# Weight halves read twice from DRAM by GpSimd's DMAs, and the residual put into PSUM ahead of the down products

## The chip, the cores and the metric

The kernel runs on one core of a Trainium2 chip. The metric is device time in microseconds (us) of one execution, lower is better. The core's engines run side by side, each through a queue of its own in a fixed order: TensorE (PE, matmuls and transposes), ScalarE (ACT), VectorE (DVE), GpSimd (POOL) and SyncE (SP), which here only issues DMAs. An instruction waits at the head of its engine's queue for what it reads or overwrites, and everything behind it on that engine waits with it. DMAs are moved by 16 DMA engines that all queues share.

## The reference

The reference is a decoder of two layers on 256 tokens of width 2048, in float32. Each layer projects the normalised x once, runs two groups of attention heads side by side (gated linear attention and stick-breaking attention), adds the output projection to x, and then adds an MLP of width 8192 with a squared ReLU:

```python
h = rms_norm(x, attn_norm)
proj = jnp.einsum('bsd,de->bse', h, w_in)
g_q, g_k, g_v, g_gate, g_lr, s_q, s_k, s_v = jnp.split(proj, COL_SPLITS, axis=-1)
...
mixed = jnp.concatenate([o_gla, o_sb], axis=-1)
x = x + jnp.einsum('bse,ed->bsd', mixed, w_o)
hm = rms_norm(x, mlp_norm)
up = jnp.square(jax.nn.relu(jnp.einsum('bsd,df->bsf', hm, w_up)))
return x + jnp.einsum('bsf,fd->bsd', up, w_down)
```

The weights `w_in`, `w_o`, `w_up` and `w_down` of both layers, some 400 MB, are read from DRAM in float32, and nearly all of the time goes into their products with 256 tokens.

## The kernel before

**Products.** A float32 product is made of three faster ones. An operand `w` is split into a high part, `w` rounded to the type fp32r, and a low part, `w` less the high part; the product is high by high, high by low and low by high (lines L1121, L1122 and L1123 in `product`, L594 to L596 in `unit`). So each matmul has three rows in the profile, on tiles `whi`, `wlo` or `dlo` (weights, high and low) and `act` (activations).

**Units and pairs.** Away from the attention the work is cut into units of 256 tokens by 1024 output columns. In a layer they are g (the gate), o twice (output projection), then four times up, up, down, down, and, ahead of each layer's attention, `iv`, `ik` and `iq`, three parts of that layer's input projection (`layer_units`). A unit runs over eight pairs; a pair is 256 rows by 1024 columns of weights, 1 MB, which SP loads into a tile `raw` in DRAM's layout (L981). ScalarE makes the high parts (L1008, `high`), VectorE the low parts (L1012, `low`), in halves of 128x1024 each.

**Fast and added pairs.** Pairs 1, 3, 5 and 6 (`FAST`) take seven products in place of eight, by Strassen and Winograd; their sums of weights are VectorE's (L840, tiles `ts`). Pairs 2 and 7 (`ADDED`) spare VectorE the low part: ScalarE writes the negated high part into a tile `dlo` (L1018, a copy with scale −1 that rounds), and a DMA of GpSimd adds `raw` onto it, from SBUF to SBUF (L1021). ScalarE makes their high part as well, so an added half costs it two instructions. There are 38 units with added pairs, 152 halves.

**PSUM and tails.** Products are summed in eight banks, called m1 to m8 by number. When a unit ends, `down_tail` or `up_tail` empties the banks. A down unit or an o unit adds its sums to the residual x, which stays in SBUF as `xb`: twelve VectorE additions on 128x512 (L840), among them those that read `xb` and write it. An up unit's tail applies the squared ReLU and turns the result for the next products (ScalarE L1185 and L1213 among others).

**What sets the order.** Inside `ordered` (called before layer 0 and once a layer), ScalarE's and VectorE's instructions are put in order by `Plan`, a list scheduler with a length for each piece of work and due times counted from TensorE's order. TensorE, SP and GpSimd keep the order in which the program adds their work. Outside it (the opening product of GV, `unit` with operands from `operand_parts`, L471 to L494; and the attention) the order is the program's. Tiles come in rings: 5 of `whi`, 4 of `wlo`, 2 of `dlo`, 5 of `raw`.

**Two places.** At the start SP loads x in four pieces between weights (L356, L309 gains, L564 weights), TensorE transposes x (L471) with idle transposes of `ident` ahead of it (L544), and ScalarE scales the result to the first operand (L481). At the end of each layer's attention ScalarE and VectorE finish a head norm (squares L662, VectorE's sum L663, statistics L386 and L387), while unit g's first weights come in.

Of the kernel before, what the change touches and what calls it, by code (L numbers as in the profile page):

```python
# [14 lines left out]
ALU = mybir.AluOpType  # L15
# [6 lines left out]
STEPS = [0, 0, 1, 1, 1, 2, 3, 1, 3, 2, 3, 3, 4, 4, 5, 5, 6, 5, 5, 6, 6, 6, 7, 7]  # L22
LOADS = [0, 1, 2, 3, 4, 5, 6, 7]
FAST = (1, 3, 5, 6)
FEWER = [0, 0, 1, 1, 1, 2, 3, 1, 3, 2, 3, 3, 4, 4, 5, 5, 6, 6, 6, 6, 7, 7], (1, 3, 6)
ADDED = (2, 7)
# [21 lines left out]
class Plan:  # L48
# [10 lines left out]
    class Piece:  # L59
        def __init__(self, engine, length, fn, deps, lag):  # L60
            self.engine, self.length, self.fn, self.lag = engine, length, fn, lag
            self.deps = deps
            self.users = []
            self.after = []
# [4 lines left out]
    def add(self, engine, length, fn, *deps, lag=0.0):  # L69
        flat = []  # L70
        for d in deps:
            flat.extend(d if isinstance(d, (list, tuple)) else [d])
        self.pieces.append(Plan.Piece(engine, length, fn, [d for d in flat if d], lag))
        return self.pieces[-1]

    def run(self):
# [25 lines left out]
        order, events, count = [], [], 0  # L102
        for p in self.pieces:
            if not p.deps:
                events.append((0.0, count, p))
                count += 1
        came = set()
        while events:
            now, _, p = heapq.heappop(events)
# [6 lines left out]
            for e in free:  # L116
                if free[e] > now + 1e-9:
                    continue
                if e in ready:
                    if not ready[e]:  # L120
                        continue
                    p = heapq.heappop(ready[e])[2]
# [6 lines left out]
                heapq.heappush(events, (free[e], count, None))  # L129
                count += 1  # L130
                for u in p.users:
# [4 lines left out]
                    if not left[u]:  # L136
                        heapq.heappush(events, (at[u], count, u))
                        count += 1
# [8 lines left out]
def trunk_kernel(  # L147
# [59 lines left out]

    ATT = ("wg", "ident16", "mask16", "tri", "nones", "gmask", "reset", "v4", "lr", "lrT", "ha", "hh", "hl", "hA", "on", "dec", "S", "kdz", "row", "bc", "eg")
    MLP = ("whi5", "dlo", "sxh", "sx", "ts", "raw2")
# [213 lines left out]
    def forms(op, i, t, tag):  # L423

        keep = tag is None
# [16 lines left out]
        def high():  # L442
            if e:
                if keep:
# [378 lines left out]
    def ordered(l, units, hT, rst, ug, gates_t, mixed=None, ons=None):  # L823
# [11 lines left out]
        RING, LOWS, ADDS, RAWS = 5, 4, 2, 5  # L835
# [11 lines left out]
        def unit_order(u):  # L847

            kind, _, n2 = units[u]
            if kind == "g":  # L850
                return [i // 2 for i in range(8)], ()
            if kind == "o":
                pairs = ((4, 5, 6, 7, 0, 1, 2, 3), (4, 5, 6, 0, 7, 1, 2, 3))[n2]
                return [j for j in pairs for _ in range(4 if j < 2 else 2)], (0, 1)
            return FEWER if u and units[u - 1][0] == "down" and kind == "iv" else (STEPS, FAST)

        def step_banks(u, j, is_fast):
# [4 lines left out]
            if kind in BIG and j in ADDED and not by_columns(u, j):  # L862
# [24 lines left out]
        def squares(n, ss):  # L887
            return add("ACT", 2 * A1, lambda: norm_squares(n, ss), x_done[n])
# [23 lines left out]
        def made(f, got, tag_fast, first):  # L912
# [9 lines left out]
            if tag_fast:  # L922
                e = add("DVE", 1.25, lambda: part(0), first)
            b = add("ACT", A1 * (2 if tag_fast else 1), lambda: part(1), e)
            return add("DVE", 1.1 if tag_fast else V1, lambda: part(2), b)

        def turned(n, h2, m, op, key, ll, sums=False):
# [4 lines left out]
            if sums and fast(i):  # L932
                box = []
                b = add("ACT", A1, lambda: box.append(scaled()), a)
                free[m] = [b]
                return made(
                    lambda: forms(op, i, box[0], None if op is hT else "sxh"), None, True, b
# [23 lines left out]
        def load(u, i):  # L961
# [4 lines left out]
            def fn():  # L966
                if x % RAWS >= RAWS - 2:
                    box.append(tmp("raw2", [P, 2, 1024], bufs=2))
# [21 lines left out]
        def by_columns(u, i):  # L990

            return units[u][0] in BIG and i in ADDED and i == unit_order(u)[0][-1]

        def high_tile():
            if len(whi) % RING == 0:
                return lambda: tmp("whi5", [P, 2, 512], F32R, bufs=1)
            return lambda: ppool.tile([P, 2, 512], F32R, tag="whi", name=nm("whi"), bufs=RING - 1)

        def parts(src, readers, deps, n=2, by_dma=False):
# [16 lines left out]
            def negated():  # L1016
                box["l"] = tmp("dlo", [P, 2, 512], F32R, bufs=ADDS)
                nc.scalar.activation(box["l"], src(), AF.Copy, scale=-1.0)  # L1018

            def add_weights():  # L1020
                nc.gpsimd.dma_start(f32(box["l"]), src(), accum_op=ALU.add)  # L1021

            if by_dma:
                m = add("ACT", A2, negated, deps, dlo[-ADDS] if len(dlo) >= ADDS else [])
                lo = add("POOL", 2.7, add_weights, m, lag=ADD)
                dlo.append([])
                readers.extend((m, lo))
            h = add("ACT", A2 if n == 2 else A1, high, deps, whi[-RING], last.get("h"))
            whi.append([])
            if not by_dma:  # L1030
                lo = add("DVE", V2 if n == 2 else V1, low, h, wlo[-LOWS], last.get("l"))
                last["l"] = lo
                wlo.append([])
                whi[-1].append(lo)
                readers.append(lo)
            last["h"] = h
            readers.append(h)
            return box, h, lo, [whi[-1], (dlo if by_dma else wlo)[-1]]

        last = {}  # L1040
        sums13 = []


        def steps(u, j, is_fast, r, ld, readers):
# [16 lines left out]

            def ext(i):
# [693 lines left out]
```

## Time and profile before

| what | before |
|---|---|
| median of 3 runs | 2133.17 us (2133.06 to 2133.46) |
| profiled execution, its own span | 2131.6 us |
| TensorE busy | 2123.5 us |
| VectorE busy | 1929.5 us |
| ScalarE busy | 1535.1 us |
| GpSimd busy | 152.1 us |
| read from DRAM | 405.12 MB |

The profile is that of one execution. A row of its groups names the line, the engine, the operation, the tiles (output from input, numbers left out), their shapes and the count; then the busy time, the mean of one in ns, and the idle time just before them with what ended most of it. A row of the timeline gives the start in us, the busy time, engine, line and tiles, and in brackets the idle time ahead of it with its releaser. A row of the waits gives engine and tile, the releaser, the sum, the count and the longest. PEld is the loading of weights into TensorE beside its matmuls. "SPq" and "POOLq" mark DMAs that these engines issue.

### The profile page before, as it was taken

The numbers are of one execution on the slowest core, as the hardware profiler recorded it, in microseconds if no ns is written. First come the engines' busy times: TensorE is split into PE (matmuls) and PEld (weight loads), VectorE is DVE, ScalarE is ACT, GpSimd is POOL, SyncE is SP. The second block draws the span as 40 slices with busy tenths as digits, with TensorE's granted clock in tenths as the row PEclk, the third lists the DMA queues.
The fourth block names the chain that finished last, engine by engine and source line by source line (L and its number), as shares of the span: only waits on it lengthen the run. The fifth ranks groups of instructions, "written<-read, shape, count | busy, mean of one in ns | idle before, by whom it ended". The sixth has DMA issues, their size and how long they took to land.

```text
span 2131.6 us, 28370 instructions
## 1 busy us (share of the span) xinstructions
PE 2123.5 (100%) x10094; PEld 1768.9 (83%) x10094; DVE 1929.5 (91%) x2598; ACT 1535.1 (72%) x1989; POOL 152.1 (7%) x210
## 2 busy tenths in 40 slices
PE   9999999999999999999999999999999999999999
PEld 7888888888888888888888888888888888888887
DVE  6988779999999999999998886799999999999998
ACT  7777666777677677677777665667876776776775
POOL 0010000000000000000000100000000000000000
PEclk9999999999999999999999999999999999999999
DMA  8975355688888888878888644657888888888886
GB/s 287 265 203 182 115 198 178 217 242 264 249 247 252 249 256 249 269 237 254 238 260 252 178 138 136 201 186 219 262 234 267 245 261 250 246 254 248 254 252 178
DMA packets 156114, 488.76 MB, mean 229 GB/s; under 512 B 9690, under 2 KB 18466, under 8 KB 155972
## 3 DMA queue, kind: packets, MB, share of 16 engines
q1 hardware_dynamic: 134084, 407.25, 55.9%
q0 software_dynamic: 21888, 79.70, 19.7%
q8 instruction: 79, 1.29, 0.2%
q14 instruction: 63, 0.52, 0.1%
HBM read 405.12 MB, written 2.10 MB: 191 GB/s over the span
## 4 chain that ended last, share of the span: by engine, by line
PE 96%; DVE 2%; ACT 1%; issue 0%; DMA 0%; DVEq 0%; ACTq 0%
PE acc L594 3%; PE acc L596 3%; PE acc L595 3%; DVE wlo L1012 0%; PE ps L1693 0%; PE ps L1686 0%; DVE wlo L577 0%; PE ps L705 0%; PE ps L1643 0%; PE ps L759 0%; PE ps L723 0%; DMA dlo<-raw 0%; DVE t L1548 0%; PE ps L471 0%; PE ps L771 0%
## 5 line engine op out<-in xcount | busy, mean ns | idle before, releaser
L1008 ACT ACTIVATE whi<-raw 128x1024 fp32r<-128x1024 f32 (+1 forms) x847 | 814.9, 976 | 344.5 <-issue 48.2
L1012 DVE TENSOR_TENSOR wlo<-raw,whi 128x1024 fp32r<-128x1024 f32 (+1 forms) x695 | 757.6, 1097 | 88.3 <-ACT whi L1008 76.0
L1021 POOL DMA_DIRECT2D dlo<-raw x152 | 129.4, 852 | 1733.7 <-ACT dlo L1018 921.1
L1008 ACT ACTIVATE whi<-ts 128x1024 fp32r<-128x1024 f32 x159 | 168.6, 1060 | 80.0 <-DVE ts L840 5.8
L1012 DVE TENSOR_TENSOR wlo<-ts,whi 128x1024 fp32r<-128x1024 f32 x159 | 193.9, 1219 | 11.1 <-ACT whi L1008 8.4
L840 DVE TENSOR_TENSOR ts<-raw 128x1024 f32<-128x1024 f32 x159 | 194.0, 1220 | 2.7 <-DMA raw<-in_w_in_dram 0.9
L1018 ACT ACTIVATE dlo<-raw 128x1024 fp32r<-128x1024 f32 x152 | 155.3, 1044 | 3.6 <-PE m__2021_9487 L1122 1.7
L594 PE MATMUL acc<-whi,act 128*128 128x512 f32 (+2 forms) x384 | 141.3, 368 | 0.0
L596 PE MATMUL acc<-whi,act 128*128 128x512 f32 (+2 forms) x384 | 136.9, 356 | 0.0
L595 PE MATMUL acc<-wlo,act 128*128 128x512 f32 (+2 forms) x384 | 136.7, 356 | 0.0
L575 ACT ACTIVATE whi<-raw 128x1024 fp32r<-128x1024 f32 (+2 forms) x98 | 88.5, 908 | 63.7 <-PE acc L596 63.0
L577 DVE TENSOR_TENSOR wlo<-raw,whi 128x1024 fp32r<-128x1024 f32 (+2 forms) x98 | 100.4, 1031 | 33.2 <-ACT whi L575 33.1
L840 DVE TENSOR_TENSOR raw<-raw 128x512 f32<-128x512 f32 x159 | 109.4, 688 | 2.7
L840 DVE TENSOR_TENSOR raw<-ts,raw 128x512 f32<-128x512 f32 x159 | 108.9, 685 | 0.7
L594 PEld LDWEIGHTS acc<-whi,act 128*128 128x128 f32 x384 | 72.6, 189 | 12.3 <-issue 3.4
L596 PEld LDWEIGHTS acc<-whi,act 128*128 128x128 f32 x384 | 72.4, 189 | 10.5
L595 PEld LDWEIGHTS acc<-wlo,act 128*128 128x128 f32 x384 | 72.6, 189 | 8.9 <-DVE wlo L577 0.2
L1213 ACT ACTIVATE act<-act,st 128x512 f32<-128x512 f32 x88 | 60.3, 712 | 25.9 <-DVE act L840 25.9
L456 DVE TENSOR_TENSOR act<-t,act 128x512 fp32r<-128x512 f32 x88 | 59.8, 683 | 0.0
L452 ACT ACTIVATE act<-t 128x512 fp32r<-128x512 f32 x88 | 54.3, 621 | 0.4 <-DVE t L440 0.3
L840 DVE TENSOR_TENSOR xb<-t,xb 128x512 f32<-128x512 f32 x40 | 27.3, 682 | 0.1
L663 DVE TENSOR_REDUCE st<-t 128x4 f32<-128x512 f32 (+1 forms) x36 | 21.8, 619 | 5.7 <-ACT t L662 5.5
(3399 smaller groups left out, 5605.6 us busy)
## 6 DMA issues: line engine op xcount, KB each, us to landing
raw<-in_w_up_dram SPq DMA_DIRECT2D x112, 1024.0 KB, 6.3
raw<-in_w_down_dram SPq DMA_DIRECT2D x112, 1024.0 KB, 6.3
raw<-in_w_in_dram SPq DMA_DIRECT2D x78, 1024.0 KB, 5.5
dlo<-raw POOLq DMA_DIRECT2D x152, 512.0 KB, 6.5
raw<-in_w_o_dram SPq DMA_DIRECT2D x32, 1024.0 KB, 5.1
raw<-in_w_up_dram SPq DMA_DIRECT2D x32, 512.0 KB, 6.7
raw<-in_w_down_dram SPq DMA_DIRECT2D x32, 512.0 KB, 6.5
raw<-in_w_in_dram SPq DMA_DIRECT2D x26, 512.0 KB, 6.4
```

The costliest lines, as they stand in the source:

```text
L456: nc.vector.tensor_tensor(d[:, :, 1, :], src, f32(d[:, :, 0, :]), ALU.subtract)
L575: newest["hi"] = nc.scalar.activation(h, r, AF.Copy).ins
L577: newest["lo"] = nc.vector.tensor_tensor(lo[:, q : q + step, :width], r, f32(h), ALU.subtract).ins
L594: nc.tensor.matmul(o, xh[:, sl], whi[:, j, :width], start=first, stop=False)
L595: nc.tensor.matmul(o, xh[:, sl], wlo[:, j, :width], start=False, stop=False)
L596: st["mm"] = nc.tensor.matmul(o, xl[:, sl], whi[:, j, :width], start=False, stop=last).ins
L840: nc.vector.tensor_tensor(dst, a, b, op)
L1008: nc.scalar.activation(box["h"][:, :n], src(), AF.Copy)
L1012: nc.vector.tensor_tensor(box["l"][:, :n], src(), f32(box["h"][:, :n]), ALU.subtract)
L1018: nc.scalar.activation(box["l"], src(), AF.Copy, scale=-1.0)
L1021: nc.gpsimd.dma_start(f32(box["l"]), src(), accum_op=ALU.add)
L1213: nc.scalar.activation(box[h][:, tt, :], box[h][:, tt, :], AF.Relu if into else AF.Copy, scale=(rr if into else st["rst"])[:, tt : tt + 1],)
```

## The change

**Added pairs.** A half of an added pair is no longer loaded by SP. GpSimd's DMAs read it from DRAM twice: once with a cast to fp32r into a tile `chi`, which is the high part, and once, after ScalarE has written the negated `chi` into `dlo`, adding the weights from DRAM onto it. So ScalarE's high instruction is gone for the 152 halves, SP issues fewer loads (by the order, 96 of 1 MB for up and for down in place of 112), GpSimd's DMAs go from 152 to 304, and the DRAM read grows by the second reading to some 485 MB. `chi` has a ring of 3, `raw` one of 3 in place of 5; GpSimd queues the next half's `chi` ahead of a half's addition (`AHEAD_BY`). The added pairs are now 2 and 4, and their two halves are no longer neighbours in the order of steps (`EACH`).

**Seeds.** In the eight down units of a layer and the second o unit (`SEEDED`), 18 in all, ScalarE copies the four residual tiles of `xb` into banks 2, 4, 3 and 8 before the unit's first products there, which then add onto them. The tail is eight VectorE instructions in place of twelve.

**The scheduler** also counts the temporary tiles `t2` now: a piece that takes one is held until one is left (`take`, `sure`, `give`).

```diff
-STEPS = [0, 0, 1, 1, 1, 2, 3, 1, 3, 2, 3, 3, 4, 4, 5, 5, 6, 5, 5, 6, 6, 6, 7, 7]
-ADDED = (2, 7)
+EACH = [0, 0, 1, 1, 1, 1, 2, 3, 3, 3, 3, 2, 5, 5, 5, 5, 4, 6, 6, 6, 6, 4, 7, 7], FAST, (2, 4)
+SEEDED = (("down", 0), ("down", 1), ("o", 1))
+CAST, AHEAD_BY = 3, 1
+RING, LOWS, ADDS, RAWS = 5, 4, 2, 3
...
-                if by_columns(u, i):
-                    for c in range(2):
-                        nc.sync.dma_start(
-                            dst[:, c, :].rearrange("p (k n) -> p k n", k=2),
-                            src[:, :, c * 512 : (c + 1) * 512],
-                        )
-                else:
-                    nc.sync.dma_start(dst, src)
+                nc.sync.dma_start(dst, src)
...
+        def rounded(u, j, s):
+            box = {}
+            sl = slice(s * 512, (s + 1) * 512)
+            src = weights(u, j)[:, :, sl] if by_columns(u, j) else weights(u, j)[:, s : s + 1, :]
...
+            def high():
+                box["h"] = tmp("chi", [P, 2, 512], F32R, bufs=CAST)
+                nc.gpsimd.dma_start(flat("h"), src)
+            def negated():
+                box["l"] = tmp("dlo", [P, 2, 512], F32R, bufs=ADDS)
+                nc.scalar.activation(box["l"], f32(box["h"]), AF.Copy, scale=-1.0)
+            def add_weights():
+                nc.gpsimd.dma_start(flat("l"), src, accum_op=ALU.add)
+            users = [[], []]
+            h = add("POOL", 1.0, high, chi[-CAST] if len(chi) >= CAST else [], lag=LAND)
+            chi.append(users[0])
+            if len(late) >= AHEAD_BY:
+                late.pop(0)()
...
+            def rest():
+                m = add("ACT", A2, negated, h, dlo[-ADDS] if len(dlo) >= ADDS else [])
+                dlo.append(users[1])
+                got[2] = add("POOL", 1.0, add_weights, m, lag=ADD)
+            late.append(rest)
...
+        def seed(m, x):
+            banks[m] = bank(m)
+            nc.scalar.activation(banks[m], x(), AF.Copy)
+        def seeded_tail(u):
...
+            seeds = {
+                m: add("ACT", A1, lambda m=m, x=x: seed(m, x), free[m], x_done.get(2 * n2 + c))
+                for m, x, c in ((2, x11, 0), (4, x21, 0), (3, x12, 1), (8, x22, 1))
+            }
```

Three places of the order of instructions, each before and after. Lines have moved: L481 is now L500, L494 is L513, L575 is L594, L1008 is L1066, L662 is L681, L386 and L387 are L402 and L403, L880 is L903. New are L1033 (the load `chi`), L1037 (the negation) and L1040 (the addition).

GpSimd's queue at the start of the program, before; `dlo` are the low parts of added halves:

```order
masks.py:197 MEMSET ident 128x128
masks.py:199 ISA
masks.py:199 AFFINE_SELECT ident<-ident 128x128
L1021 DMA dlo_457<-raw_400 128x1024
L1021 DMA dlo_467<-raw_400 128x1024
L1021 DMA dlo_648<-raw_558 128x1024
```

and after:

```order
masks.py:197 MEMSET ident 128x128
L1033 DMA chi_398<-in_w_in_dram 128x1024
masks.py:199 ISA
masks.py:199 AFFINE_SELECT ident<-ident 128x128
L1033 DMA chi_400<-in_w_in_dram 128x1024
L1040 DMA dlo_406<-in_w_in_dram 128x1024
L1033 DMA chi_413<-in_w_in_dram 128x1024
L1040 DMA dlo_408<-in_w_in_dram 128x1024
```

The first load of `chi` now stands between the two instructions that make `ident`, and two loads and the first addition come right behind.

ScalarE at the start, before; `act` is the operand of the opening product, `whi` its weights' high parts:

```order
L241 ACT_TABLE_LOAD
L481 ACTIVATE act_122<-ps_109,gcol_a 128x256 x2
L481 ACTIVATE act_127<-ps_114,gcol_a 128x256 x2
L575 ACTIVATE whi_151<-raw_146 128x512 x2
L575 ACTIVATE whi_159<-raw_146 128x512 x2
```

and after:

```order
L257 ACT_TABLE_LOAD
L1037 ACTIVATE dlo_406<-chi_398 128x1024
L1037 ACTIVATE dlo_408<-chi_400 128x1024
L500 ACTIVATE act_122<-ps_109,gcol_a 128x256 x2
L500 ACTIVATE act_127<-ps_114,gcol_a 128x256 x2
L594 ACTIVATE whi_151<-raw_146 128x512 x2
L594 ACTIVATE whi_159<-raw_146 128x512 x2
```

Two negations, which wait for the first two loads of `chi`, moved to the head of the queue, ahead of the first operand.

ScalarE at the end of layer 0's attention, before; `raw_2917` holds unit g's first weights:

```order
L784 ACTIVATE act_2712<-ps_2834 128x512
L1008 ACTIVATE whi_622_2925<-raw_2917 128x1024
L662 ACTIVATE t_591_2847<-act_2712 128x512
L386 ACTIVATE st_2851<-st_2850 128x4
L387 ACTIVATE st_2851<-st_2851 128x4
L880 ACTIVATE act_2896<-acc_2610,st_393 128x512
L1008 ACTIVATE whi_2930<-raw_2917 128x1024
```

and after:

```order
L803 ACTIVATE act_2697<-ps_2819 128x512
L681 ACTIVATE t_585_2832<-act_2697 128x512
L402 ACTIVATE st_2836<-st_2835 128x4
L403 ACTIVATE st_2836<-st_2836 128x4
L1037 ACTIVATE dlo_2912<-chi_2904 128x1024
L1037 ACTIVATE dlo_2914<-chi_2906 128x1024
L1066 ACTIVATE whi_619_2917<-raw_2902 128x1024
L903 ACTIVATE act_2881<-acc_2595,st_393 128x512
```

The first high of unit g moved from ahead of the squares to behind the statistics and two negations. Layer 1 has the same rows at its place.

More of the change, by code (lines that the diff above doesn't have):

```diff
@@ L1028, in parts @@
             h = add("ACT", A2 if n == 2 else A1, high, deps, whi[-RING], last.get("h"))
             whi.append([])
[L1030 to L1035, printed above, removed]
+            lo = add("DVE", V2 if n == 2 else V1, low, h, wlo[-LOWS], last.get("l"))
+            last["l"] = lo
+            wlo.append([])
@@ L1036, in parts @@
+            whi[-1].append(lo)
+            readers.append(lo)
             last["h"] = h
             readers.append(h)
-            return box, h, lo, [whi[-1], (dlo if by_dma else wlo)[-1]]
+            return box, h, lo, [whi[-1], wlo[-1]]
         last = {}
         sums13 = []
+        chi, late, made_halves = [], [], {}
+        every = [
+            (u, k, j, order[:k].count(j))
+            for u in range(len(units))
+            for order, _, by_dma in [unit_order(u)]
+            for k, j in enumerate(order) if j in by_dma
+        ]
@@ L1129, in down_tail @@
         def down_tail(u):
[L1130 to L1131 removed]
+            n2 = units[u][2]
             x11, x21, x12, x22 = (
```

270 lines of the change are left out of this document (179 added, 91 removed).

## The prediction

> **What bounds the kernel now.** I read first the page's head and busy times, then the windows over single stretches, then the waits of TensorE, and last the timeline where the windows or waits leave a gap.
>
> ```profile
> span 2131.6 us, 28370 instructions
> PE 2123.5 (100%) x10094; PEld 1768.9 (83%) x10094; DVE 1929.5 (91%) x2598; ACT 1535.1 (72%) x1989; POOL 152.1 (7%) x210
> ```
>
> Windows of the start, the first unit of the list scheduler and a long stretch of the MLP (columns: window, its length, busy us and instructions of PE, PEld, DVE, ACT, POOL, granted clock, DMA share, GB/s):
>
> ```profile
> 0.00:10.00 10.00, 7.90 (x32) 6.77 (x33) 2.41 (x6) 4.69 (x9) 0.70 (x6) 1.00 0.74 223
> 10.00:20.00 10.00, 10.00 (x53) 8.46 (x52) 7.63 (x14) 8.04 (x20) 0.00 (x0) 1.00 1.04 394
> 34.00:75.00 41.00, 40.49 (x174) 31.81 (x173) 39.28 (x57) 32.38 (x40) 3.64 (x4) 1.00 0.84 239
> 700.00:1100.00 400.00, 400.00 (x1814) 332.18 (x1813) 380.28 (x487) 302.01 (x372) 31.92 (x38) 1.00 0.83 248
> ```
>
> All the waits of TensorE that the profile counts:
>
> ```profile
> PE ps L544 <- POOL ident masks.py:199: 1.4, 1, 1.4
> PE ps L705 <- DVE act L668: 1.1, 2, 0.5
> PE ps L471 <- DMA xb<-in_x_dram: 0.7, 1, 0.7
> PE m__79_428 L1122 <- DMA dlo<-raw: 0.3, 1, 0.3
> PE m__4043_18997 L1121 <- DVE xb L840: 0.2, 1, 0.2
> ```
>
> TensorE is the bound: from 700 to 1100 us it is busy 400.00 of 400.00 us, at the full granted clock, and outside that it waits 3.7 us in all. The matmuls are the same in number and shape before and after. So no saving on ScalarE, VectorE or SP can shorten the time by more than TensorE's idle, 2131.6 − 2123.5 = 8.1 us, most of which lies at the very start. What can happen is that something arrives late. I therefore price the work saved at nothing and look for what becomes late.
>
> **The work taken away.** Rows of the page's groups for the instructions that change in number (the DMA's row is its issue on GpSimd):
>
> ```profile
> L1008 ACT ACTIVATE whi<-raw 128x1024 fp32r<-128x1024 f32 (+1 forms) x847 | 814.9, 976 | 344.5 <-issue 48.2
> L1021 POOL DMA_DIRECT2D dlo<-raw x152 | 129.4, 852 | 1733.7 <-ACT dlo L1018 921.1
> L1018 ACT ACTIVATE dlo<-raw 128x1024 fp32r<-128x1024 f32 x152 | 155.3, 1044 | 3.6 <-PE m__2021_9487 L1122 1.7
> L840 DVE TENSOR_TENSOR xb<-t,xb 128x512 f32<-128x512 f32 x40 | 27.3, 682 | 0.1
> ```
>
> ScalarE loses the 152 highs of the added halves (152 × 0.976 = 148 us); it gains 72 copies of the residual into PSUM, at about 0.58 us (the PSUM copy of L1185 below) 42 us. VectorE loses 72 × 0.682 = 49 us from the tails of 18 units. GpSimd issues 304 DMAs in place of 152, 0.85 us each, on an engine that is busy 7% of the time. Both lie beside a full TensorE: worth 0. The few early waits that more room on these engines may remove are 0.5 us (40.49 of 41.00 busy in 34:75) and the 0.2 us at the last unit: −0.7 us.
>
> **The transfers.** The queues' rows (packets, MB, share of 16 engines) and the landing times of two kinds of DMA (KB, us from issue to landing):
>
> ```profile
> q1 hardware_dynamic: 134084, 407.25, 55.9%
> q0 software_dynamic: 21888, 79.70, 19.7%
> raw<-in_w_up_dram SPq DMA_DIRECT2D x112, 1024.0 KB, 6.3
> dlo<-raw POOLq DMA_DIRECT2D x152, 512.0 KB, 6.5
> ```
>
> A half is 0.524 MB. As an SP load it takes all 16 engines 0.559 × 2131.6 / 407.25 × 0.524 = 1.53 us; as an accumulate 0.197 × 2131.6 / 79.70 × 0.524 = 2.76 us. The trace has no casting load from DRAM (`chi`); I bound it by these two, 1.53 and 2.76 us, and take the lower, since it reads DRAM and writes SBUF as the SP load does and reads no destination. The accumulate now reads DRAM in place of SBUF; I leave it at 2.76. A half then costs 4.29 us as before, at most 5.52; at four halves in a unit of some 41 us the DMA share goes from 0.83 to between 0.83 and 0.95. Under 1: worth 0 in the steady part, if each half is asked for early enough. GpSimd queues one half ahead, so within a 41 us unit halves are wanted every 7 us or so; reckoning the chain (`chi` landing, negation 1.04 us, accumulate landing) at 6.5 us a landing, the last accumulate is there about 3.6 us before its product. I take 0. Upper end: with a cast as dear as an accumulate, a wait of some 0.5 us in each of the 38 units that have added pairs, 19 us.
>
> Three raw buffers in place of five: an SP load now waits for the last reader three loads back. In the order of a unit pair 5's load waits for pair 0's last read, some 2.7 us into the unit; with 6.3 us to land it is there at 9 us, and wanted at 12 to 14 us: 0.
>
> **The seeds.** A seeded unit may not start a bank before ScalarE has copied the residual into it. At the end of a down unit's predecessor, near 2000 us:
>
> ```profile
> 1994.56 0.58 ACT L1185 ACTIVATE act<-m__3813_17928 128x512 f32<-128x512 f32 x1
> 1997.56 0.68 DVE L840 TENSOR_TENSOR act<-m__3799_17862,act 128x512 f32<-128x512 f32 x1
> 2000.55 0.68 DVE L840 TENSOR_TENSOR act<-m__3802_17875,act 128x512 f32<-128x512 f32 x1
> 2000.87 0.39 PE L1121 MATMUL m__3868_18198<-whi,act 128*128 128x512 f32 x1
> 2002.23 0.39 PE L1121 MATMUL m__3871_18211<-whi,act 128*128 128x512 f32 x1
> ```
>
> Bank 2 is read out at 1998.24 and written again at 2000.87, a slack of 2.6 us; bank 4 at 2001.23 and 2002.23, 1.0 us. A copy of 0.58 us fits both, so 0. If ScalarE is in another instruction of 1 us, bank 4 is late by half a microsecond: at most 18 × 0.5 = 9 us, the upper end.
>
> **The start.** The first rows of GpSimd's queue now are `chi` loads, and ScalarE's first two instructions are the negations of two of them, ahead of the operand that opens the first product. Rows of SP's queue, ScalarE and TensorE at the start of before:
>
> ```profile
> 0.82 0.95 SPq L356 DMA_DIRECT2D xb<-in_x_dram  x2
> 1.82 0.46 SPq L309 DMA_DIRECT2D t<-in_attn_norm_dram  x1
> 2.32 1.85 SPq L564 DMA_DIRECT2D raw<-in_w_in_dram  x4
> 4.21 0.43 SPq L356 DMA_DIRECT2D xb<-in_x_dram  x1
> ...
> 6.54 1.57 ACT L481 ACTIVATE act<-ps,gcol_a 128x256 fp32r<-128x256 f32 x4 [4.44 <-DVE gcol_a L319]
> ...
> 1.44 1.97 PE L544 MATMUL ps<-ident 128*128 128x128 f32 x8 [1.44 <-POOL ident masks.py:199]
> ...
> 6.21 3.04 PE L544 MATMUL ps<-ident 128*128 128x128 f32 x13
> 8.90 0.78 PE L594 MATMUL acc<-whi,act 128*128 128x512 f32 x1
> ...
> 12.40 1.03 PE L471 MATMUL ps<-ident,xb 128*128 128x128 f32 x8
> ```
>
> Two things can hold it up. First GpSimd and ScalarE: `chi` issues of 0.85 us stand before and behind the two instructions that make `ident`, which comes 0.85 later; the 8 warm transposes then end at 4.26, and x's transposes, at 4.07 before, lose 0.2, which lies inside what follows. The second `chi` is issued at about 2.2 us; if it lands as GpSimd's DMAs do in the middle of the kernel, 6.5 us less the 1.4 by which a load takes the engines shorter than an accumulate (2.76 − 1.33, below), at 7.3, its negation ends at 8.4, where the operand began at 6.54: +1.8. (Had it landed by 4.4 us, nothing would be lost.) Second the shared engines: the windows show 2.23 MB moved by 10 us at 223 GB/s, and the second piece of x, with 2.1 MB ahead of it or in it, comes just then; TensorE transposes it at 12.40, a slack of 2.4 us. Now three `chi` (3 × 1.33 us, 0.524 MB at the 394 GB/s of 10:20) and two accumulates (2 × 2.76) can share the engines with it: 9.5 us. If they take turns, x comes at 19.5 and TensorE is held by 19.5 − 12.4 = +7.1 us. If SP's stream goes first, 2.1 MB of x and gains and 3.15 MB of weights, 17.6 us by the same rates with the 0:10 window's, the two `chi` and the negation end at 17.6 + 2 × 1.33 + 1.04 = 21.3, and ScalarE's operand is late by +14.8. Between 0 and +14.8 I take +7.1, as both queues have work from 2 us on and nothing in the trace shows one of them held back.
>
> The Trainium skill, "DMA: Bandwidth & Descriptors", section "Queues, rings and completion order", says that each DMA engine goes round its queues packet by packet; by that rule the two streams take turns and the term is 7.1, not 14.8. No run here shows it yet. The Trainium skill, "TensorE: Matmul & The Clock Gate", "Part 1: The HAM clock gate", has the array fall to half rate after about 3.4 us of idleness; the trace agrees in the start, where 13 transposes took 3.04 us and 8 later ones 1.03. By that page, as an estimate, a hold of 7 us would cost half of 3.4, some 1.7 us, more, and the sum would read 2143.5.
>
> **The two ends of attention.** `chi` shares memory with the attention's tiles, so each `ordered` begins with fresh halves. In both layers two negations stand ahead of the first high of unit g (the order above). The timeline of before there:
>
> ```profile
> 284.64 1.05 ACT L1008 ACTIVATE whi<-raw 128x1024 fp32r<-128x1024 f32 x1
> 285.59 0.62 ACT L662 ACTIVATE t<-act 128x512 f32<-128x512 f32 x1
> ...
> 288.03 0.21 ACT L387 ACTIVATE st<-st 128x4 f32<-128x4 f32 x1
> ...
> 285.73 1.23 DVE L1012 TENSOR_TENSOR wlo<-raw,whi 128x1024 fp32r<-128x1024 f32 x1 [2.02 <-ACT whi L1008]
> ...
> 289.63 0.39 PE L1121 MATMUL m__629_2942<-whi,act 128*128 128x512 f32 x1
> 289.86 0.39 PE L1122 MATMUL m__629_2942<-wlo,act 128*128 128x512 f32 x1
> ...
> 1347.71 0.39 PE L1121 MATMUL m__2660_12490<-whi,act 128*128 128x512 f32 x1
> ```
>
> The high at 284.64 was 5 us ahead of TensorE. Now it follows L387's counterpart. Without high and low ahead of them, the squares of L662 and VectorE's sum come about 1.5 us earlier, so the statistics end at 288.24 − 1.5 = 286.7; two negations (2.09) end at 288.8, the high at 289.85, the low 1.23 later at 291.1, where the product read it at 289.86: +1.25, less what the matmul before it covers, +1.1. Were the statistics not earlier, +2.6. Twice: +2.2 (2 to 5). The negations themselves wait for `chi` loads that are issued when the attention's last tiles are free, some 280 us, landing at about 286.7: just in time.
>
> **The sum.** 2131.6 + 7.1 + 2.2 − 0.7 = 2140.2. This execution's span stands 1.6 us below the median of 2133.17 (2133.06 to 2133.46), so 2141.8 us, 0.4% slower. What a measurement can tell here is about 0.2%, 4.3 us: 2128.9 to 2137.4 is no change.
>
> **The rivals.** B, SP's stream goes first at the start: 2131.6 + 14.8 + 2.2 − 0.7 + 1.6 = 2149.5. For it: SP issues half a dozen loads before GpSimd's first; against it: loads and accumulates ran beside each other all through the MLP. C, not slower: the first two `chi` land by 4 to 5 us and x is not pushed past its slack, so the start costs nothing: 2131.6 + 2.2 − 0.7 + 1.6 = 2134.7. For it: in 0:10 the DMA share was only 0.74 and the accumulates come late, after a landing and a negation; it decides when the start costs under 2.8 us. D, the cast is as dear as the accumulate or the chain of three steps too slow: the start costs 5 × 2.76 − 2.4 = 11.4, that is 2146, and with up to 0.5 us in 38 units 2165, its middle about 2152. For it: the 6.5 us to landing is a median with little behind it (slack 3.6 us); against it: a share of at most 0.95.
>
> **The chances.** The likeliest case, the turns at the start, 0.45 (its own range 2138 to 2147); C 0.22; D 0.20; B 0.13. Faster by over 0.2% would need 4.3 us of TensorE's 8.1 us idle, of which 0.7 is within reach: 0.03. Same takes most of C: 0.20. Slower 0.77. The range leaves out the lowest part of C and the upper half of D: 2134 to 2156.
>
> **What would show it.** ScalarE's first instructions after would be two `dlo<-chi` that wait for DMAs, and the first `act<-ps` after 6.54 us; TensorE's wait on `ps<-xb` would be about 7 us. In unit g of both layers the first product with `wlo` would come 1 to 2 us after the statistics' old place, with a wait on VectorE's low. In 700:1100 TensorE would still be at 400 of 400 with a DMA share of 0.83 to 0.95. If it shows waits on `dlo` or on `xb` copies into the banks instead, D or the seeds' upper end is right. A `chi` load that lands in 3 us at the start would make the forecast too high; a share at 1.0 too low.

## The result and the profile after

The changed kernel takes 2150.07 us (median of four runs, 2148.3 to 2156.37) against 2133.28 us before: the ratio is 1.0085, with an interval of 1.0070 to 1.0099. That is slower by 0.85%, inside the forecast's range and twice as far from the kernel before as its 2141.8 us. The runs before lie within 0.4 us of each other, those after within 8 us. The profiled execution after has a span of 2146.6 us.

The head of the page, the two queues and the landing times of the changed kernel:

```profile
span 2146.6 us, 28212 instructions
PE 2127.6 (99%) x10094; PEld 1768.6 (82%) x10094; DVE 1886.1 (88%) x2526; ACT 1436.8 (67%) x1909; POOL 234.6 (11%) x362
...
q1 hardware_dynamic: 103076, 327.55, 44.3%
q0 software_dynamic: 43776, 159.40, 31.2%
...
raw<-in_w_up_dram SPq DMA_DIRECT2D x96, 1024.0 KB, 10.2
chi<-in_w_up_dram POOLq DMA_DIRECT2D x64, 512.0 KB, 6.8
dlo<-in_w_up_dram POOLq DMA_DIRECT2D x64, 512.0 KB, 9.4
```

VectorE lost 43 us of work and ScalarE 98 us, and neither moved the end. TensorE has the same 10094 rows and 4 us more of busy time (products right after a wait take longer); its idle time grew from 8.1 to 19.0 us. The additions land 9.4 us after their issue where they took 6.5, and SP's loads of 1 MB 10.2 where they took 6.3.

TensorE's waits after:

```profile
PE acc L613 <- ACT whi L594: 3.7, 1, 3.7
PE ps L563 <- POOL ident masks.py:199: 2.5, 1, 2.5
PE ps L490 <- DMA xb<-in_x_dram: 1.4, 1, 1.4
PE m__3274_15522 L1202 <- DMA dlo<-in_w_down_dram: 1.1, 1, 1.1
PE m__3882_18394 L1202 <- DMA dlo<-in_w_down_dram: 1.1, 1, 1.1
...
PE m__626_2935 L1202 <- DVE wlo L1070: 0.8, 1, 0.8
PE m__2619_12388 L1202 <- DVE wlo L1070: 0.8, 1, 0.8
...
PE m__1279_6067 L1202 <- DMA dlo<-in_w_down_dram: 0.6, 1, 0.6
```

Three groups are new or longer: the start (the first three rows), the first low of unit g in each layer (0.8 us twice), and additions that come late (`dlo`). How much each costs is read at marks that both programs have. TensorE's order between them holds the same work, so the difference of two times is the delay collected so far. The marks are the end of the opening product on ScalarE, the first gate product of each layer's attention on TensorE, and the last matmul. Before:

```profile
34.36 0.60 ACT L880 ACTIVATE act<-acc 128x512 f32<-128x512 f32 x1 [3.13 <-PE acc L596]
...
186.84 1.13 PE L1536 MATMUL ps<-lrT,wg 17*128 17x256 f32 x4
1223.36 1.13 PE L1536 MATMUL ps<-lrT,wg 17*128 17x256 f32 x4
2127.19 0.39 PE L1123 MATMUL m__4048_19021<-whi,act 128*128 128x512 f32 x1
```

and after:

```profile
42.20 0.60 ACT L903 ACTIVATE act<-acc 128x512 f32<-128x512 f32 x1 [3.63 <-PE acc L615]
...
195.28 1.13 PE L1676 MATMUL ps<-lrT,wg 17*128 17x256 f32 x4
1235.12 1.13 PE L1676 MATMUL ps<-lrT,wg 17*128 17x256 f32 x4
2142.10 0.39 PE L1203 MATMUL m__3972_18829<-whi,act 128*128 128x512 f32 x1
```

The delay is 42.20 − 34.36 = 7.8 us at the end of the opening, 8.4 at the first gate product, 11.8 at the second and 14.9 at the end. So half of it is collected in the first 42 us and the rest in small pieces.

**The start.** ScalarE, TensorE and the queues of the changed kernel (the last three rows are the window from 13.80 to 17.30 us, in the columns of the prediction's windows, and the queues' shares in the first 24 us):

```profile
8.32 1.06 ACT L1037 ACTIVATE dlo<-chi 128x1024 fp32r<-128x1024 f32 x1 [6.22 <-DMA chi<-in_w_in_dram]
10.73 1.06 ACT L1037 ACTIVATE dlo<-chi 128x1024 fp32r<-128x1024 f32 x1 [1.35 <-DMA chi<-in_w_in_dram]
11.69 1.55 ACT L500 ACTIVATE act<-ps,gcol_a 128x256 fp32r<-128x256 f32 x4
...
13.81 0.51 PE L613 MATMUL acc<-whi,act 128*128 128x512 f32 x1 [3.70 <-ACT whi L594]
15.56 0.63 PE L613 MATMUL acc<-whi,act 128*128 128x512 f32 x1
15.99 0.63 PE L614 MATMUL acc<-wlo,act 128*128 128x512 f32 x1
18.59 1.04 PE L490 MATMUL ps<-ident,xb 128*128 128x128 f32 x8
23.77 1.09 PE L490 MATMUL ps<-ident,xb 128*128 128x128 f32 x8 [1.40 <-DMA xb<-in_x_dram]
...
13.80:17.30 3.50, 3.27 (x8) 2.39 (x9) 3.28 (x6) 2.35 (x5) 0.00 (x0) 0.55 1.07 262
...
q1 hardware_dynamic: 2543, 4.25, 53.3%
q0 software_dynamic: 720, 2.62, 42.0%
```

The two negations at the head of ScalarE's queue wait for `chi` until 8.3 and 10.7 us, and the first operand is made at 11.69 in place of 6.54. The first matmul comes at 13.81 in place of 8.90, 4.9 us late. TensorE has then waited 3.7 us and runs its next products 0.43 us apart (15.56 to 15.99) where 0.23 is its pace, at a granted clock of 0.55: 13.81 to 18.59 takes 4.8 us where 8.90 to 12.40 took 3.5, another 1.3 us, of which 0.2 is a wait for a low part. The third piece of x adds 1.4. The two queues share the engines, 53% and 42%, and landings stretch: SP's first weights (256 KB) take 8.1 us where they took 5.2 (and 5.4 in e2 below, which holds the `chi` loads back).

**The first low of unit g.** At the end of layer 0's attention:

```profile
295.15 1.99 ACT L1037 ACTIVATE dlo<-chi 128x1024 fp32r<-128x1024 f32 x2
297.04 1.04 ACT L1066 ACTIVATE whi<-raw 128x1024 fp32r<-128x1024 f32 x1
...
298.12 1.23 DVE L1070 TENSOR_TENSOR wlo<-raw,whi 128x1024 fp32r<-128x1024 f32 x1 [1.57 <-ACT whi L1066]
...
299.40 0.50 PE L1202 MATMUL m__626_2935<-wlo,act 128*128 128x512 f32 x1 [0.76 <-DVE wlo L1070]
```

The two negations run on ScalarE from 295.15, the high follows at 297.04 and the low at 298.12, and TensorE waits for it. From 8.51 (298.14 against 289.63, the product ahead) the delay goes to 9.54 (299.40 against 289.86).

**A late addition.** GpSimd's queue and TensorE near 690 us:

```profile
684.76 0.55 POOL L1033 DMA_DIRECT2D chi<-in_w_down_dram  x1 [5.69 <-PE m__1284_6092 L1202]
686.84 0.85 POOL L1040 DMA_DIRECT2D dlo<-in_w_down_dram  x1 [1.53 <-ACT dlo L1037]
...
696.67 0.50 PE L1202 MATMUL m__1279_6067<-dlo,act 128*128 128x512 f32 x1 [0.65 <-DMA dlo<-in_w_down_dram]
```

The `chi` load of the next half and the negation of this half wait for products of the same finished half, since `chi` has three buffers and `dlo` two. So the load is issued 2 us ahead of the addition, in the same queue, and the addition lands 9.8 us after its issue (696.67 − 686.84), later than TensorE wants it.

### The profile page after: what moved, and what is told of

It is laid out like the page before. It is cut to its first block, busy times and chain, and to the rows that moved or that the text cites. A ratio compares the mean times of both kernels' runs of the same rounds, so it can differ in the third digit from the quotient of the medians.

```text
span 2146.6 us, 28212 instructions
## 1 busy us (share of the span) xinstructions
PE 2127.6 (99%) x10094; PEld 1768.6 (82%) x10094; DVE 1886.1 (88%) x2526; ACT 1436.8 (67%) x1909; POOL 234.6 (11%) x362
## 3 DMA queue, kind: packets, MB, share of 16 engines
q0 software_dynamic: 43776, 159.40, 31.2%
## 4 chain that ended last, share of the span: by engine, by line
issue 47%; PE 42%; POOL 6%; DMA 2%; DVE 1%; ACT 1%; SPq 0%; POOLq 0%
POOL dlo L1040 3%; PE acc L613 3%; PE acc L615 3%; PE acc L614 3%; POOL chi L1033 2%; DMA dlo<-in_w_down_dram 1%; DMA xb<-in_x_dram 1%; DMA raw<-in_w_up_dram 1%; DVE wlo L596 0%; PE ps L724 0%; PE ps L1833 0%; PE ps L778 0%; PE ps L1783 0%; PE ps L1826 0%; PE ps L742 0%
## 5 line engine op out<-in xcount | busy, mean ns | idle before, releaser
L1066 ACT ACTIVATE whi<-raw 128x1024 fp32r<-128x1024 f32 (+1 forms) x695 | 654.6, 958 | 285.1 <-DVE raw L858 121.2
L1037 ACT ACTIVATE dlo<-chi 128x1024 fp32r<-128x1024 f32 x152 | 160.3, 1056 | 132.4 <-DMA chi<-in_w_down_dram 18.3
L1066 ACT ACTIVATE whi<-ts 128x1024 fp32r<-128x1024 f32 x159 | 168.5, 1060 | 57.3 <-DVE ts L858 16.7
L594 ACT ACTIVATE whi<-raw 128x1024 fp32r<-128x1024 f32 (+2 forms) x98 | 88.1, 906 | 65.1 <-PE acc L615 64.1
L1033 POOL DMA_DIRECT2D chi<-in_w_up_dram x64 | 35.4, 554 | 780.1 <-PE m__820_3916 L1203 142.2
L1033 POOL DMA_DIRECT2D chi<-in_w_down_dram x64 | 35.4, 554 | 517.3 <-PE m__982_4673 L1203 34.5
L613 PEld LDWEIGHTS acc<-whi,act 128*128 128x128 f32 x384 | 72.6, 189 | 16.4 <-ACT whi L594 4.3
L615 PEld LDWEIGHTS acc<-whi,act 128*128 128x128 f32 x384 | 72.8, 189 | 10.6
L614 PEld LDWEIGHTS acc<-wlo,act 128*128 128x128 f32 x384 | 72.9, 190 | 9.4 <-DVE wlo L596 0.5
L1040 POOL DMA_DIRECT2D dlo<-in_w_down_dram x64 | 54.7, 855 | 62.9 <-ACT dlo L1037 60.0
L1040 POOL DMA_DIRECT2D dlo<-in_w_up_dram x64 | 54.8, 856 | 52.0 <-ACT dlo L1037 50.3
## 6 DMA issues: line engine op xcount, KB each, us to landing
raw<-in_w_up_dram SPq DMA_DIRECT2D x96, 1024.0 KB, 10.2
```

The lines of the kernel that those rows point to most:

```text
L594: newest["hi"] = nc.scalar.activation(h, r, AF.Copy).ins
L613: nc.tensor.matmul(o, xh[:, sl], whi[:, j, :width], start=first, stop=False)
L614: nc.tensor.matmul(o, xh[:, sl], wlo[:, j, :width], start=False, stop=False)
L615: st["mm"] = nc.tensor.matmul(o, xl[:, sl], whi[:, j, :width], start=False, stop=last).ins
L1033: nc.gpsimd.dma_start(flat("h"), src)
L1037: nc.scalar.activation(box["l"], f32(box["h"]), AF.Copy, scale=-1.0)
```

## The experiments

Each line of this table is a kernel made from the changed one. The last four columns are the delay at the marks above against the kernel before (first times of the same rows in each trace, subtracted). The kernel before had medians of 2133.05 to 2133.16 us beside them.

| run | median us (lowest to highest) | ratio to before, interval | opening | gate 0 | gate 1 | end |
|---|---|---|---|---|---|---|
| changed kernel | 2150.07 (2148.3 to 2156.4) | 1.0085 (1.0070 to 1.0099) | 7.8 | 8.4 | 11.8 | 14.9 |
| e1 negations late | 2144.48 (2139.3 to 2147.5) | 1.0051 (1.0035 to 1.0067) | 2.5 | 3.9 | 9.0 | 14.1 |
| e2 chi after x | 2142.51 (2140.1 to 2147.0) | 1.0046 (1.0031 to 1.0061) | −0.2 | 1.7 | 5.6 | 7.3 |
| e3 first weights first | 2145.55 (2144.0 to 2151.4) | 1.0067 (1.0051 to 1.0084) | 7.1 | 8.8 | 10.9 | 10.6 |
| e4 three dlo | 2201.90 (2198.0 to 2207.7) | 1.0325 (1.0307 to 1.0342) | 7.5 | 11.4 | 39.0 | 64.7 |
| e5 start and first weights | 2140.35 (2138.9 to 2141.9) | 1.0034 (1.0023 to 1.0046) | 0.2 | 0.8 | 3.7 | 7.5 |
| e6 four chi | 2139.97 (2137.4 to 2142.8) | 1.0033 (1.0020 to 1.0046) | 0.1 | 0.8 | 5.0 | 7.2 |
| e7 addition ahead | 2136.23 (2134.6 to 2139.8) | 1.0016 (1.0007 to 1.0026) | −0.3 | 0.3 | 2.0 | 2.5 |
| e8 addition from SBUF | 2141.32 (2140.3 to 2142.4) | 1.0039 (1.0024 to 1.0054) | −0.3 | 0.3 | 5.7 | 9.0 |

### e1 and e2: what holds the start

e1 queues the first two negations behind the opening's last operand on ScalarE; e2 also makes GpSimd wait for the last piece of x before its first `chi` load:

```diff
+                with tc.issue_after(opened_by) if l < 0 and len(dlo_made) < 2 else nullcontext():
+                    nc.scalar.activation(box["l"], f32(box["h"]), AF.Copy, scale=-1.0)
...
+            x_here.append(nc.gpsimd.tensor_copy(stat(1), xb[3][:, 1, 511:512]).ins)
...
+                with tc.issue_after(x_here[0]) if l < 0 and len(chi_made) < 2 else nullcontext():
+                    nc.gpsimd.dma_start(flat("h"), src)
```

> Only the two negations at the head of ScalarE's queue are moved behind the opening's operands; the chi loads stay where they are. If the shared DMA engines are what holds the start, the first product comes near 9 us as before, but the pieces of x come late all the same, and the start keeps 3 to 5 of its 7.8 us: about 2146 us. If ScalarE's hold is the cause, and x is late only because the two additions follow the negations so early, the start loses at most 1 us and the time is about 2142.5 us.

> As the run before, and GpSimd also waits for the last piece of x before it issues the first chi load. Both theories expect the start of before, first product at 9 us and no wait on x, about 2142 us; what differs from the run before is the part of the shared engines.

In e1 the delay at the end of the opening falls from 7.8 to 2.5 us, in e2 to −0.2. Both expectations of e1 miss in part: the hold of ScalarE is 5.3 of 7.8 (the first additions move back with the negations that they follow), and the shared engines cost 2.7, not 3 to 5 and not under 1. e1's rows show what is left:

```profile
9.49 0.49 PE L613 MATMUL acc<-whi,act 128*128 128x512 f32 x1 [0.83 <-ACT whi L594]
...
14.38 1.09 PE L490 MATMUL ps<-ident,xb 128*128 128x128 f32 x8 [0.78 <-DMA xb<-in_x_dram]
...
10.74 0.63 ACT L594 ACTIVATE whi<-raw 128x512 fp32r<-128x512 f32 x1 [1.30 <-DMA raw<-in_w_in_dram]
```

Weights (1.3 us) and x (0.8 us) are late by the `chi` loads alone. The medians follow: 5.6 and 7.6 us less than the changed kernel.

### e3: the first low of unit g

```diff
                 m = add(
                     "ACT", A2, negated, h, dlo[-ADDS] if len(dlo) >= ADDS else [],
+                    firsts[:1] if l >= 0 and len(dlo) < 2 else [],
                 )
```

`firsts[0]` is unit g's first low.

> Only at the end of each layer's attention: the first two negations wait for unit g's first low, so that its first high stands ahead of the statistics again. Theory: the two waits on the first low (0.8 us each) go, 2 us in all, about 2148 us. Rival: the statistics or the chi loads, not the order, set that point; then the waits stay and the time is 2150 us.

```profile
293.42 1.05 ACT L1069 ACTIVATE whi<-raw 128x1024 fp32r<-128x1024 f32 x1
...
298.41 0.39 PE L1204 MATMUL m__623_2927<-whi,act 128*128 128x512 f32 x1
298.64 0.39 PE L1207 MATMUL m__623_2927<-wlo,act 128*128 128x512 f32 x1
```

The high is back ahead of the squares, and the product with the low follows the one with the high after 0.23 us: no wait in either layer. The order of ScalarE's queue was the cause. The run's median fell by 4.5 us, more than these 2 us; its spread of 7 us does not tell the difference.

### e4 to e8: the late additions

e4 has three `dlo` buffers in place of two (`ADDS`).

> Three dlo buffers in place of two. Theory: an addition is issued late because its negation waits for the product two halves back, and lands 9.5 us later; with a third buffer it starts up to 7 us earlier, the waits on dlo go (3.2 us in the profiled run) and with them the spread of the runs: 2146 to 2147 us, all runs within 1 us. Rival: the additions are late since the 16 engines have no room; then the waits on dlo and the spread of 8 us stay.

The run refutes both: 52 us slower than the changed kernel. By the order of its instructions, the addition of a half now stands ahead of the next half's `chi` load in 107 of 152 cases (3 before), so that a load waits until the negation of the half ahead is done. GpSimd's queue, and ScalarE's waits for `chi` in that run:

```profile
715.09 0.88 POOL L1040 DMA_DIRECT2D dlo<-in_w_down_dram  x1 [6.65 <-ACT dlo L1037]
715.64 0.89 POOL L1033 DMA_DIRECT2D chi<-in_w_down_dram  x1
...
ACT dlo L1037 <- DMA chi<-in_w_up_dram: 144.3, 38, 8.1
...
ACT dlo L1037 <- DMA chi<-in_w_in_dram: 44.4, 14, 6.9
ACT dlo L1037 <- DMA chi<-in_w_down_dram: 42.3, 24, 4.8
```

ScalarE stands 231 us in front of negations whose `chi` has not landed (51 us in the changed kernel), and what is queued behind them there comes late. The engines have room all the same: the 64 additions of up units land in 5.7 us (median). Load, negation and addition had become one chain, and the wait sat on an engine that TensorE needs.

e5 takes the start of e2 and the order of e3 together, as a base. e6 adds a fourth `chi` buffer, so that a load is two halves ahead; it is still queued just ahead of an addition that the same product sets free. e7 queues that load behind the addition:

```diff
-CAST, AHEAD_BY = 3, 1
+CAST, AHEAD_BY = 4, 1
...
+                behind = x_here if l < 0 and len(chi_made) < 2 else acc_ins
+                with tc.issue_after(behind[-1]) if behind else nullcontext():
+                    nc.gpsimd.dma_start(flat("h"), src)
```

e8 is e5 with another source of the addition:

```diff
-                nc.gpsimd.dma_start(flat("l"), src, accum_op=ALU.add)
+                nc.gpsimd.dma_start(f32(box["l"]), f32(box["h"]), accum_op=ALU.add)
```

> The start of e2 and the order of e3 together. If start (+7.8 us) and the two ends of attention (+0.9 each) are all that is lost beside late additions, TensorE is level with the kernel before until the late additions come, and the time is 2133 us plus 2 to 6: 2135 to 2139 us, with a spread of some us between runs. If something else is lost, it is above 2140.

> e5 with a fourth chi buffer: a chi load still goes into GpSimd's queue just ahead of an addition that the same product sets free, but two halves ahead of its use. If the addition lands late because that load is in front of it, its 9.5 us to landing stay, and the waits on dlo with them: as e5, 2135 to 2139 us. If chi itself is what comes late, the waits go: 2134 us.

> e6 with the addition in front of that chi load in GpSimd's queue. Theory: it lands in 5 to 7 us in place of 9.5, the waits on dlo and the spread go, 2133 to 2134 us. Rivals: it lands late since it reads DRAM, or since the 16 engines have no room; then 9 to 10 us to landing and 2135 to 2139 us as in e5.

> e5 with the addition reading chi from SBUF in place of the weights in DRAM, so that the low part of the added halves is left out (the product is coarser there); the size and the place in the queue stay. If reading DRAM is what makes the addition land at 9.5 us, it lands at 6.5 as before the change, and the time is 2133 to 2134 us. If the chi load in front is, the 9.5 us stay within 1 us and the time is as in e5.

e5 is level with the kernel before at the first gate product (0.8 us) and loses the rest in the units that follow. At 2140.35 us it is above 2140, which by its expectation means that something else is lost: beside five listed waits on `dlo` (2.0 us), its trace has two waits of TensorE on seeds (0.7 and 0.4 us). e6 is no different (2139.97): the `chi` loads were not what came late. The additions' landing (least, median, most) in e6, and the two queues' order there:

```profile
683.50 0.56 POOL L1034 DMA_DIRECT2D chi<-in_w_down_dram  x1 [5.86 <-PE m__1288_6115 L1216]
684.36 0.86 POOL L1044 DMA_DIRECT2D dlo<-in_w_down_dram  x1 [0.30 <-ACT dlo L1040]
...
DMA to landing us min/median/max: 5.5/9.9/12.9
```

and in e7:

```profile
685.78 0.86 POOL L1046 DMA_DIRECT2D dlo<-in_w_down_dram  x1 [6.00 <-ACT dlo L1041]
686.34 0.86 POOL L1035 DMA_DIRECT2D chi<-in_w_down_dram  x1
...
DMA to landing us min/median/max: 5.2/8.8/15.7
```

Only the order of the two DMAs differs between e6 and e7. The addition lands 1.1 us sooner, no wait on `dlo` is left among TensorE's (3.4 us in e6), and the median falls by 3.7 us to 2136.23 us. That the load in front is part of what made the additions late is shown; that they would land in 5 to 7 us was wrong, and `chi` itself now takes 10.2 us to land where it took 6.9. The Trainium skill, "DMA: Bandwidth & Descriptors", section "Two DMAs through the same engine are not ordered", says that descriptors of one queue start in order but overlap; the two landing times of e7 fit that, though no row shows single descriptors.

What keeps the additions at 8.8 us was not tested, but the traces point at SP's queue. In the kernel before, 13 of the 152 additions have a DMA of SP issued between 2 us ahead of them and 1 us behind, and these land in 9.5 us (median), the other 139 in 6.5. In the changed kernel 116 of 152 have one, in e7 117. In e4, of the additions without a `chi` load in the 2.5 us ahead of them, the 81 without such a DMA land in 5.7 us and the 49 with one in 8.8. A load of SP that starts at the same time is therefore a second cause that fits as well as the load in front, and the change made it the usual case.

In e8 the addition from SBUF lands at 9.6 us as the one from DRAM does, and its waits on `dlo` (4.7 us) are no smaller. So reading DRAM does not make the additions late.

### e9 to e11: the seeds, and room on VectorE

e9 is e7 with seeds in the first of each two down units only. The last down unit's tail does not store its half of the output there, which leaves four stores of 256 KB out.

> e7 with seeds in the first of each two down units only (8 units in place of 18); the other down units and o get the tail of twelve VectorE additions back. If the seeds cost TensorE nothing and spare only hidden work, the time is that of e7, 2135 to 2138 us; if a seed is waited for in each unit (up to 0.5 us), ten fewer units make it 3 to 5 us shorter; if VectorE's relief had paid, it is longer.

It takes 2135.97 us (2133.8 to 2138.3), but with the missing stores its span ends 2.8 us after its last matmul in place of 4.4, so it counts as some 2137.5, and its last matmul is 4.9 us behind the kernel before (2.5 in e7). Within the spread of the two that is the same. No wait on a seed is among TensorE's in either, nor in the changed kernel's trace. So the seeds of the ten units neither cost nor gain within the noise. One wait on `dlo` is back in e9's trace (1.3 us): the order of e7 makes such waits rare, not impossible. They are not free in every execution: the traces of e1, e4, e5 and e8 have one to four waits on seeds, 0.9 to 2.1 us in all.

e10 gives the 16 down units a fifth fast pair (pair 7, ahead of the second half of pair 4, which now ends the unit) on the base of e5; e11 does so on the base of e7 with four `whi` buffers. In both the sums of the down products with that pair come out otherwise than the reference's; all instructions are issued, so the runs price the order of work alone.

```diff
-FAST_OF = {"sxh": FAST, "sx": FAST}
+FAST_OF = {"sxh": FAST, "sx": (1, 3, 5, 6, 7)}
...
+FIVE = [0, 0, 1, 1, 1, 1, 2, 3, 3, 3, 3, 2, 5, 5, 5, 5, 6, 6, 6, 6, 4, 7, 7, 7, 7, 4], (1, 3, 5, 6, 7), (2, 4)
+OWN = {("down", 0): FIVE, ("down", 1): FIVE}
```

> e5 with pair 7 of the 16 down units made fast as well, which takes 3 matmuls of 0.227 us from each: 10.9 us less for TensorE, 120 instructions more for VectorE, which is then near 92% busy. If VectorE's room is real, 2140.4 - 10.9 = 2129 to 2131 us, faster than the kernel before; if the stages of a down unit have no room on VectorE, its waits eat the gain: 2138 us or more.

> The same five fast pairs with the fourth chi buffer and the addition ahead in the queue (e7), paid for in memory by one whi buffer less. If both hold, 2136.2 - 10.9 = 2125 to 2127 us; if four whi buffers are too few, waits on whi take more than that back.

They take 2216.92 and 2241.06 us. VectorE is 89% and 88% busy, so it isn't short of room over all. In e10 TensorE waits for a seed at the start of a down unit eight times, 3.6 us each. The copy itself waits for VectorE's tail, and the product after it takes 0.79 us where 0.39 is usual:

```profile
1067.72 0.60 ACT L1265 ACTIVATE m__2020_9458<-xb 128x512 f32<-128x512 f32 x1 [1.73 <-DVE xb L859]
...
1068.38 0.79 PE L1213 MATMUL m__2020_9458<-whi,act 128*128 128x512 f32 x1 [3.60 <-ACT m__2020_9458 L1265]
```

A seed can only be written when the tail ahead has read its bank. With a fast pair near the unit's end the banks are read out later, and the copy then lies on TensorE's path. The profiled run of e10 is 72.9 us longer than that of e5 (2212.1 and 2139.2), and its rows account for it: TensorE is idle 44.4 us more (55.8 and 11.4), of which the seeds are 28.8 and seven waits on `xb` from the same tail 14.3, and it is busy 28.5 us more although it has 48 products fewer. The granted clock shows why: 0.50 from 1068.3 to 1071.5 us, behind one of these waits, and 0.986 in the mean where e5 has 1.000. So the expectation's second case holds: the stages of a down unit have no room on VectorE. e11 has the same waits (eight of 3.6 us on seeds, seven of 2.9 us on `xb`), and its waits on `whi`, 6.8 us, are the smaller part.

## Why the prediction came out as it did

- **What bounds, and the worth of the work saved.** Right: TensorE is busy 2127.6 of 2146.6 us, and 141 us less work on ScalarE and VectorE shortened nothing. The −0.7 us for early waits did not come: from the end of the opening to the first gate product the delay grows by 0.6 (7.8 to 8.4).
- **The start, +7.1.** The size was right (7.8), the working was not, so that the two agree is luck. The step failed that says "x comes at 19.5 and TensorE is held". It set three loads and two additions of GpSimd against the second piece of x; the third load and the additions were issued only from 9.69 us on, and the piece landed at 13.5 us, in time for its transposes (18.59, no wait). It was ScalarE that held TensorE, behind a `chi` load that landed at 10.7 us where the step on ScalarE reckoned 7.3. That step's +1.8 is 5.2 (11.69 against 6.54). Rival B's order is refuted: it has the second negation end at 21.3 us, which began at 10.73. That B's sum, 2149.5, is the nearest to the measured time is chance. C is refuted too, which asked for a landing by 4 to 5 us. The engines do go to both streams: the rule of the Trainium skill on the turns of the queues ("DMA: Bandwidth & Descriptors", "Queues, rings and completion order") agrees with the shares of 53% and 42%. Its rule on the clock gate ("TensorE: Matmul & The Clock Gate", "Part 1: The HAM clock gate") fits the products 0.43 us apart at a granted clock of 0.55 after a wait of 3.7 us, and the cost was 1.3 us where 1.7 was estimated. The transposes ahead of that wait, however, already ran slowly (13 in 3.04 us); the fall itself is seen in e10, where products are 0.23 us apart up to a wait of 3.6 us and 0.43 after it.
- **The two ends of attention, +2.2.** Right in mechanism and size: 0.9 to 1.0 us each by the delay on both sides, and 0 with the order undone (e3). The statistics came earlier as forecast (295.04 against 288.03 + 8.4).
- **The transfers, 0.** This is the term that was mis-sized. The step reckoned the chain "at 6.5 us a landing" with 3.6 us of slack; the additions took 9.4 us, which is 2.9 more, and the slack was all but gone. Part of D's mechanism, then, came on top of the likeliest case: 3.0 us of waits in the profiled run, and by e7 against e6 some 3.7 us in the medians. The price of the cast was near the lower bound as taken: both kinds of DMA together use 0.312 × 2146.6 / 159.40 × 0.524 = 2.20 us of the engines a half (mean of the two), which leaves 1.64 for the load if the addition still takes 2.76, as no row shows by itself. With a DMA share of 0.84 in 700:1100 the engines' time was not the limit. The order in the queue explains 1.1 us of the longer landing (9.9 in e6, 8.8 in e7); the rest goes, in the traces, with SP's loads that start beside the additions, and no run tests this.
- **The seeds, 0.** Right for the profiled run of the changed kernel; in those of e1, e4, e5 and e8 they cost 0.9 to 2.1 us. The room is small: with the longer unit of e10 each of eight seeds is waited for.
- **The three raw buffers, 0.** Not tried with more. No wait of TensorE on `wlo` in the middle of the kernel speaks for loads of SP that come late. But the step asked only whether these loads come in time, not what they start beside; whether the shorter ring is what brings them together with the additions stays open.
- **What stays open.** The forecast was 8.3 us too low, and the pieces add up: 7.8 for the start, 1.9 for the two ends, 3.7 for the queue's order and 3 that are left, 16.4 of 16.8 us. With the first three undone (e7) 2.5 us at the last matmul and 3 us in the medians remain, in small waits at several places, and a spread of 5 us between runs where the kernel before has 1 to 2. No version here beats the kernel before.

## What to carry to other kernels

When the matrix engine is full, work taken off the others is worth nothing, and what a change costs lies in what its new waits stand in front of: an instruction that waits for a DMA at the head of an engine's queue delays everything behind it, at a start, at a change of stage, or all through. When two DMAs of one queue become ready by the same event, put the one that is wanted sooner in front, and size the time to landing for the queue as it will then be, and for the loads of other queues that will start beside it, not from the trace of a kernel where that DMA went alone. A buffer more can be worse than none if it lets a scheduler turn the order of a queue round.

## What the runs showed of the hardware

An accumulating DMA of 512 KB took 6.5 us to land (median of 139 in the kernel before) where no DMA of SP was issued beside it, and 9.5 us where one was (13). In the changed kernel, mostly behind a casting load issued 0.5 to 2.3 us earlier, it took 9.6 us, and in e7, just ahead of one, 8.8; from SBUF or from DRAM made no difference (9.6 in e8 and in e5). Loads of 1 MB on the other queue went from 6.3 to 10.2 us with the same share of the engines in use (0.83 and 0.84 in 700:1100), and with a shorter ring of raw buffers. After a wait of 3.6 us TensorE's products were 0.43 us apart, at a granted clock of 0.50, where they had been 0.23 apart (e10). And ScalarE can write a PSUM bank onto which matmuls then add, at 0.58 us for 128x512; TensorE's waits on such copies were none in the changed kernel's trace, 2.1 us in all in e1's and eight of 3.6 us in e10's.
